# w_out of blocks 2 and 3 as one product of seven block products, in a stated order

## The chip, the cores and the metric

The kernel runs on one core of one Trainium2 chip. The metric is the device time of one launch in microseconds (us). Below, PE is the tensor engine (matmuls and transposes), ACT the scalar engine, DVE the vector engine, POOL the GpSimd engine and SP the sync engine, whose queue issues nearly all transfers (DMA). Matrix operands lie in SBUF as tiles of 128 partitions; matmuls accumulate in PSUM, of which the kernel uses four tiles of two banks at a time.

## The reference, cut to what matters

One layer of a hybrid decoder block on x of 2048 rows by 1024 columns, float32:

```
h   = rmsnorm(x, norm_mix_g)
u   = h @ w_in                                   # 1024 -> 3584 columns
gate_b, gate_c, v, x_r, g = split(u)             # 512, 512, 512, 1024, 1024
y_conv = gate_b * conv3(gate_c * v)              # 512 columns
y_rnn  = rg_lru(conv4(x_r)) * gelu(g)            # 1024 columns, a scan over the rows
y   = concat[rmsnorm(y_conv, g_norm_conv), rmsnorm(y_rnn, g_norm_rnn)]
x   = x + y @ w_out                              # 1536 -> 1024 columns
h   = rmsnorm(x, norm_mlp_g)
x   = x + relu(h @ w_mlp_in)^2 @ w_mlp_out       # 1024 -> 4096 -> 1024
out = rmsnorm(x, final_norm_g)
```

Each rmsnorm divides a row by the root of its mean square, so y_conv and y_rnn each carry one factor per row (rA and rB below) beside the gain per column.

## The kernel before

**Numbers.** Each float32 operand is split into a rounded high part and a low part (`split_into`: ACT copies to the high part, line 177, DVE subtracts it for the low part, line 178). A product of two operands is three matmul passes, high by high, high by low, low by high (`passes`).

**Blocks and pairs.** The 2048 rows are four blocks of 512 rows, in two pairs: blocks 0 and 1, then blocks 2 and 3. A large product over a pair can be computed as seven block products in place of eight: the two blocks are the two row halves, and the other two dimensions are halved as well; some operands are then sums and differences of quarters. The order of the seven is (1, 2, 6, 5, 7, 3, 4) throughout (`ORDER`). The kernel before does this for both MLP products of each pair (classes `Up`, line 838, and `Down`, line 956) and for w_in in the second pair (class `In`, a subclass of `Up`, so its matmuls stand at line 838 too).

**First pair.** For blocks 0 and 1 the mixers are computed one after the other (`mixers`), each followed by `w_out_rows` (the y_rnn part of y @ w_out) and `w_out_conv` (the y_conv part). Both run at line 259, in groups of row tiles of 128 rows. Weight splits are written to DRAM (`put_by`, `cache`) and read back later. While the first pair runs, a background generator, `prepare_sums`, makes the sums of quarters of w_in that the second pair needs, a piece at each call of `step`: its DVE operations are at lines 1236 to 1247 and at 178, and the results go to DRAM. Calls of `step` stand in `col_unit`, in the first pair's up products, and in its down products as long as the number s of the 1024-row slice is below 3.

**Second pair.** `mixers2` runs the 49 products of w_in (steps n = 0 to 48, seven for each of x0, g0, x1, g1, c, v, b) with the recurrence in eight chains beside them (class `Chain`: conv, split, gates, tanh, decay, scan, times, out, add; a chain starts every four steps). In `out`, ACT squares a finished y_rnn tile and the tile is sent to DRAM on the ACT queue (`spill_y`, line 1311). The first chain's `out` is in step 12, the last one's in step 40; sums of squares go to accA and accB. After step 48 follow, block by block, `w_out_rows(2)`, `w_out_conv(2)`, `w_out_rows(3)` and `w_out_conv(3)`: y tiles are read back, split with their gain (`split_y`, lines 579 and 580), multiplied, and the result is added to x as `x += po * r` with the row factor rB (line 1579) or rA (line 1607). A row factor comes from `stats`, matmuls of the sums of squares with a column of ones (line 599), and a few small operations on DVE and one on ACT (`rstd_of`).

**Row norm and turn.** A row tile whose x is complete is normed for the MLP by `norm_tile`: two squares with accumulation on ACT (line 395), small DVE operations, a root on ACT (line 377), more small ones, two multiplications on DVE (line 401). `turn` then transposes the tile with eight PE transposes (line 1586) and ACT copies it out. From the transposed tiles come the MLP's row operands: H1 and H2 from block 2 (`split_first`), H5 and H6 from both blocks (`rest`), later H7, H3 and H4 (`later_operands`).

**What sets the order.** In `mixers2` PE, ACT and DVE run in the order of the program (`manual_schedule` names the three). In `w_out_conv` of the last block of a pair and in the MLP only PE is so ordered. Everywhere else, and for the SP queue always, a planner orders the instructions by program order and readiness when the kernel is built. Each engine executes its own list in order.

Of the kernel before, what the change touches and what calls it, by code (L numbers as in the profile page):

```python
# [1 line left out]

# [12 lines left out]
P = 128  # L15
SEQ = 2048
D = 1024
# [46 lines left out]
def block_kernel(  # L64
# [28 lines left out]
    sp = ctx.enter_context(tc.tile_pool(name="sp", bufs=4))  # L93
    dp = ctx.enter_context(
# [1161 lines left out]

    def step():
        with tc.issue_after(made_at["sp"]):
            next(background, None)
# [17 lines left out]
    def mixers2(b, H, rest):  # L1277
# [9 lines left out]
        yB = [[None] * 4 for _ in range(2)]  # L1287
        stt, ts, tt = V.scalar_tensor_tensor, V.tensor_scalar, V.tensor_tensor
# [25 lines left out]
        class Chain:  # L1314
# [143 lines left out]
        def complete(at_n, kind, k, f, n, t, ps):  # L1458
# [33 lines left out]
            else:  # L1492
# [7 lines left out]
                yA[n][pr] = spill_y(u)  # L1500
# [16 lines left out]
        last = PORDER[-1]  # L1517
        for n in range(-IN_AHEAD, len(seq)):
# [10 lines left out]
            pieces = todo.pop(n, [])  # L1529
            for fn, *args in pieces:  # L1530
                fn(*args)
# [3 lines left out]
            if nm == last and i == 7:  # L1535
                ready = [split_y(refill("y", yB[0][pr]), "g_norm_rnn", 2 * pr) for pr in range(2)]
            if nm == last and i == 3:
                load_unit(cursor[0])
                load_x(b, (0,))
            if nm == last and i == 4:  # L1540
                load_x(b, (1,))
        halves = [[acc[0][:, n : n + 1, :] for n in range(2)] for acc in (accA, accB)]
        return yA, [ready + yB[0][2:], yB[1]], *halves

    def w_out_rows(b, ysB, accB, during, late=None):
        po = [psum("po") for _ in range(NT)]
        held = []
        for pr in range(4):
            w = take("oB%d" % pr, ahead=1 if pr == 1 else OUT_AHEAD)
            y = ysB[pr]  # L1550
            if pr < 2:
                y2 = ysB[pr + 2]
                if b >= PAIRED:
                    y2 = refill("y", y2)
                ysB[pr + 2] = split_y(y2, "g_norm_rnn", 2 * pr + 4)
# [8 lines left out]
            if pr == 1 and late:  # L1564
                late(po[3].rearrange("p h (k q) -> p (h k) q", q=P))
# [52 lines left out]
    background = prepare_sums()  # L1618
# [47 lines left out]

    for b in range(0, NB, 2):
        if b < PAIRED:
# [23 lines left out]
            ysA, ysB, accA, accB = mixers(b + 1, h, early)  # L1692
        else:
            xr0, xr1, xt2 = hs["r"]

            def rest(n):
                if n == 0:
                    half_gates(0)
                    split_pair(5, xr0[:2])
                if n == 22:  # L1700
                    half_gates(1)
                later_operands(n + 3, xr0, xr1, xt2)

            with tc.manual_schedule(
                engines={nc.tensor.engine, nc.scalar.engine, nc.vector.engine}
            ):
                yA2, yB2, rA2, acc2 = mixers2(b, H, rest)
            elsewhere.clear()
            ysA = []

            def during(pr):
                if pr > 1:
                    ysA.append(split_y(refill("y", yA2[0][pr - 2]), "g_norm_conv", 2 * pr - 4))

            w_out_rows(b, yB2[0], acc2[0], during)
            ysB = [refill("y", d) for d in yB2[1][:2]]
            load_x(b + 1)
            raw0 = [temp("raw0") for _ in range(4)]
            ysB = [split_y(y, "g_norm_rnn", 2 * pr) for pr, y in enumerate(ysB)] + yB2[1][2:]
            xs = w_out_conv(b, ysA, stats(rA2[0], 512, "A"), 2, lambda t, xs: turn(xs, t, raw0))  # L1720
            ysA = [refill("y", d) for d in yA2[1]]
# [201 lines left out]
```

## Time and profile before

| | us |
|---|---|
| median of 3 runs (lowest to highest) | 2144.68 (2143.64 to 2146.54) |
| the profiled execution, its own time | 2147.37 |
| span of that execution, first to last instruction | 2145.6 |
| PE busy | 2119.6 |
| DVE busy | 1557.5 |
| ACT busy | 1065.8 |

The profile lists instructions with the time from the start of the span. Overlapping matmuls count once in a busy time, and one matmul's own duration (about 390 ns for 512 columns) is longer than the distance between two of them, since they are pipelined. A line such as "PE tps L1586 <- DVE xs L401: 6.9, 1, 6.9" says that line 1586 on PE stood idle once, for 6.9 us, until line 401 on DVE was done. A "windows" row gives, for a stretch of time, the busy time of each engine, the clock that PE was granted (1.00 is full) and the share of the DMA engines' time that was in use.

In the profiled execution w_in of the second pair runs from 1087.44 to 1376.96 us, w_out of blocks 2 and 3 from there to 1525.94 us, and the second pair's MLP to the end; between 1525.94 and 1538.59 us the last two turns stand between up products. The first pair's down products run from 782.80 to 1087.44 us.

### The profile page before, as it was taken

How to read it: one execution, taken by the hardware profiler on the slowest of the kernel's cores; microseconds unless marked ns; L12 is line 12 of the kernel's file. 1: busy time of each engine (PE TensorE's matmuls, PEld its weight loads, DVE VectorE, ACT ScalarE, POOL GpSimd, SP SyncE). 2: the span in 40 equal slices, each digit the busy share in tenths (PEclk: the TensorE clock that was granted, in tenths of full speed). 3: DMA queues.
4: the chain of work that ended last, by engine and by line, in shares of the span. 5: the costliest groups of instructions: out<-in, count | busy, mean ns of one | idle time of the engine just before them, and what ended most of it. 6: DMA issues, size and time to landing. Idle time of an engine off the chain costs nothing.

```text
span 2145.6 us, 25180 instructions
## 1 busy us (share of the span) xinstructions
PE 2119.6 (99%) x9464; PEld 1742.9 (81%) x9464; DVE 1557.5 (73%) x1826; ACT 1065.8 (50%) x1376; POOL 41.8 (2%) x62
## 2 busy tenths in 40 slices
PE   9999999999999999999999999989999999999998
PEld 7888888788888888888887777878888888888886
DVE  6889547858766779988985678534876666887776
ACT  6884357626555545433456686213564333333344
POOL 0000000000000000000000100000000000000000
PEclk9999999999999999999999999999999999999999
DMA  9988988752577678764384547866335355844432
GB/s 332 325 316 297 337 327 324 276 180 99 186 275 274 244 280 328 283 211 145 112 319 167 186 177 246 322 245 257 115 128 187 118 191 201 326 164 154 135 124 79
DMA packets 197721, 482.48 MB, mean 225 GB/s; under 512 B 15200, under 2 KB 79712, under 8 KB 197600
## 3 DMA queue, kind: packets, MB, share of 16 engines
q1 hardware_dynamic: 195328, 474.07, 61.2%
q10 hardware_dynamic: 2272, 6.82, 0.8%
q8 instruction: 74, 1.21, 0.2%
q14 instruction: 47, 0.39, 0.1%
HBM read 324.59 MB, written 156.24 MB: 224 GB/s over the span
## 4 chain that ended last, share of the span: by engine, by line
PE 87%; DVE 6%; ACT 4%; DMA 2%; issue 1%; SPq 0%; POOL 0%; ACTq 0%; DVEq 0%; POOLq 0%
PE up L838 37%; PE dn L956 27%; PE po L259 12%; PE ps_x L232 2%; PE ps_g L232 2%; PE ps_c L232 1%; PE tps L1586 1%; PE dn L975 1%; DVE v L705 1%; ACT gi L681 1%; DVE xr L638 1%; PE start_x L499 1%; ACT r L678 1%; PE start_x L232 1%; PE start_g L232 1%
## 5 line engine op out<-in xcount | busy, mean ns | idle before, releaser
L838 PE MATMUL up<-H,w_hi 128*128 128x512 f32 x2576 | 796.2, 390 | 3.9 <-ACT xr_in L1467 3.7
L838 PEld LDWEIGHTS up<-H,w_hi 128*128 128x128 f32 x2576 | 482.7, 188 | 109.3 <-issue 4.4
L838 PE MATMUL up<-H,w_lo 128*128 128x512 f32 x1288 | 501.7, 389 | 0.0
L956 PE MATMUL dn<-w_hi,z_hi 128*128 128x512 f32 x864 | 336.1, 389 | 0.0
L956 PE MATMUL dn<-w_lo,z_hi 128*128 128x512 f32 x864 | 336.1, 389 | 0.0
L956 PE MATMUL dn<-w_hi,z_lo 128*128 128x512 f32 x864 | 336.1, 389 | 0.0
L838 PEld LDWEIGHTS up<-H,w_lo 128*128 128x128 f32 x1288 | 242.1, 188 | 50.9 <-DVE w_lo L178 0.3
L177 ACT CAST z_hi<-z 128x1024 fp32r<-128x1024 f32 x112 | 118.1, 1054 | 326.5 <-PE dn L956 283.0
L178 DVE TENSOR_TENSOR w_lo<-w,w_hi 128x1024 fp32r<-128x1024 f32 x156 | 190.0, 1220 | 90.5 <-PE dn L956 36.7
L177 ACT CAST w_hi<-w 128x1024 fp32r<-128x1024 f32 x156 | 162.7, 1049 | 156.4 <-PE up L838 63.9
L956 PEld LDWEIGHTS dn<-w_hi,z_hi 128*128 128x128 f32 x864 | 162.2, 188 | 33.7
L956 PEld LDWEIGHTS dn<-w_hi,z_lo 128*128 128x128 f32 x864 | 162.2, 188 | 33.6
L956 PEld LDWEIGHTS dn<-w_lo,z_hi 128*128 128x128 f32 x864 | 162.2, 188 | 33.5
L178 DVE TENSOR_TENSOR z_lo<-z,z_hi 128x1024 fp32r<-128x1024 f32 x112 | 136.3, 1217 | 21.0 <-ACT z_hi L177 21.0
L988 DVE TENSOR_TENSOR x<-dn,x 128x1024 f32<-128x1024 f32 x108 | 131.6, 1219 | 23.2 <-PE dn L956 20.2
L259 PE MATMUL po<-w_lo,y_hi 128*128 128x512 f32 x384 | 119.3, 392 | 1.2 <-DVE w_lo L178 1.2
L259 PE MATMUL po<-w_hi,y_hi 128*128 128x512 f32 x384 | 120.1, 396 | 0.3 <-DVE ys_B L607 0.3
L259 PE MATMUL po<-w_hi,y_lo 128*128 128x512 f32 x384 | 119.7, 393 | 0.0
L259 PEld LDWEIGHTS po<-w_lo,y_hi 128*128 128x128 f32 x384 | 72.6, 189 | 17.1 <-DVE w_lo L178 1.7
L259 PEld LDWEIGHTS po<-w_hi,y_lo 128*128 128x128 f32 x384 | 72.5, 190 | 15.5 <-DVE y_lo L580 0.4
L259 PEld LDWEIGHTS po<-w_hi,y_hi 128*128 128x128 f32 x384 | 71.6, 190 | 14.6 <-DVE ys_B L607 0.5
L850 ACT COPY snap<-up 128x1024 f32<-128x1024 f32 x48 | 48.7, 1014 | 63.0 <-PE up L838 62.6
(344 smaller groups left out, 2962.1 us busy)
## 6 DMA issues: line engine op xcount, KB each, us to landing
z<-d_z SPq DMA_DIRECT2D x112, 512.0 KB, 4.7
w_hi<-d_w SPq DMA_DIRECT2D x79, 512.0 KB, 6.6
w_lo<-d_w SPq DMA_DIRECT2D x79, 512.0 KB, 6.1
w<-in_w_mlp_in_dram SPq DMA_DIRECT2D x64, 512.0 KB, 5.8
d_z<-snap SPq DMA_DIRECT2D x64, 512.0 KB, 3.2
d_z<-z SPq DMA_DIRECT2D x48, 512.0 KB, 3.4
w<-in_w_mlp_out_dram SPq DMA_DIRECT2D x48, 512.0 KB, 6.0
d_w<-w_hi SPq DMA_DIRECT2D x40, 512.0 KB, 6.2
```

The lines of the kernel that those rows point to most:

```text
L177: nc.scalar.copy(hi, src)
L178: return (lo_engine or V).tensor_tensor(lo, src, hi.bitcast(F32), SUB).ins
L232: nc.tensor.matmul(ps[:, j, lo:hi], ws[k // 4][:, k % 4, j * P : (j + 1) * P], hs[:, k, lo:hi], start=k == 0 and i == 0, stop=k == KD - 1 ...
L259: nc.tensor.matmul(ps[:, half, :], ys[:, j, t * P : (t + 1) * P], ws[j][:, 0, half * 512 : (half + 1) * 512], start=first and i == 0, stop ...
L499: nc.tensor.matmul(start_x[:, j], w[a][k // 4][:, k % 4, j * P : (j + 1) * P], h[c][:, k], start=k == 0 and n == 0, stop=k == KD - 1 and n ...
L638: V.scalar_tensor_tensor(xr[:, j, :], xr_in[:, j, k : k + TB], par("rnn_conv_w", 8 * k + c), xr[:, j, :], MUL, ADD,)
L678: nc.scalar.activation(r[own, j, :], pr_[own, e, :], AF.Sigmoid, bias=par("b_a", c)[own])
L681: nc.scalar.activation(gi[own, j, :], pr_[other, e, :], AF.Sigmoid, bias=par("b_x_swapped", c)[other])
L838: nc.tensor.matmul(ps[:, j, :], ws[:, k, j * P : (j + 1) * P], hs(k), start=i in (1, 2, 5) and k == 0 and n == 0, stop=k == 3 and n == len ...
L850: nc.scalar.copy(t, ps)
L956: nc.tensor.matmul(ps[t // 2][:, t % 2, :], zs[:, p, t * P : (t + 1) * P], ws[:, p, :], start=i in (1, 2, 5) and a == 0 and p == 0 and n == 0,
L988: V.tensor_add(xt[b, th, dh], ps[th], xt[b, th, dh])
```

## The change

The 1536 columns of y for blocks 2 and 3 times w_out become one product of seven block products. The row halves are the blocks, the halves of the inner dimension are three groups of 256 each (`OUT_ROWS`: two of y_rnn, one of y_conv), the output is halved into 512 columns. One block product is 4 row tiles x 3 groups x 2 x 3 passes = 72 matmuls of 512 columns, so the seven are 504, where the four functions before had 576.

- Since sums over both parts of y need one factor per row, y_conv is multiplied by rA/rB (computed as rA * rB * (mean square of y_rnn + eps)), spread over the partitions by a matmul (`diagonal`, `spread`), and the whole result is added to x with rB. The gains go into the tiles themselves: for y_rnn in `Chain.out`, two ACT multiplications in place ahead of the transfer; for y_conv together with the row factor.
- The sums of w_out for products 4 to 7 are made by a second background generator, `prepare_out_sums`, after the first one; four more calls of `step` are allowed, in the first two products of s = 3.
- `pair_before_mlp` holds everything from `mixers2` to the MLP with PE, ACT and DVE in program order. The factor rB of both blocks is computed in step 42, y is read back in steps 44 and 45, and the first splits are in steps 46 to 48. The y_conv tiles stay in SBUF.
- Norms and turns move: block 2's norms into product 3, its turns into product 7, block 3's norms and H1, H2 and the first two MLP weight splits into product 4; all four turns of block 3 go between the first up products of the MLP (`turns_at`), where two were.

The new functions and the changed places, cut:

```diff
-    for b in range(NB):
-        for nm in UNITS if b < PAIRED else ():
+    for b in range(PAIRED):
+        for nm in UNITS:
...
+    OUT_ROWS = (("oB0", "oB1", "oA0"), ("oB2", "oB3", "oA1"))
+    def prepare_out_sums():
...
+        for g in range(3):
+            b12, b11 = load(g, 0, 1), load(g, 0, 0)
+            yield
+            b22 = load(g, 1, 1)
+            yield
+            t3 = temp("t3", W)
+            tt(t3, b22, b12, SUB)
+            tt(b12, b12, b11, SUB)
+            yield
+            tt(b22, b22, b12, SUB)
+            hi = split(t3)
+            yield
+            put(7, g, hi, t3)
+            b21 = load(g, 1, 0)
+            hi = split(b12)
+            yield
+            put(5, g, hi, b12)
+            tt(b21, b21, b22, SUB)
+            hi = split(b22)
+            yield
+            put(6, g, hi, b22)
+            hi = split(b21)
+            yield
+            put(4, g, hi, b21)
...
                 s, v = s_of.pop(self.key), v_of[self.key]
                 square(s, v)
+                for j in range(2):
+                    nc.scalar.activation(
+                        s[:, j, :], s[:, j, :], AF.Copy, scale=par("g_norm_rnn", 2 * pr + j)
+                    )
                 yB[n][pr] = spill_y(s)
...
-                yA[n][pr] = spill_y(u)
+                yA[n][pr] = u
...
-    background = prepare_sums()
+    background = chain(prepare_sums(), prepare_out_sums())
...
+    class WOut:
+        def load(self, i, g):
+            row = []
+            for n in range(2):
+                t = wtile("w_o", (P, 2, TB), F32R)
+                if i > 3:
+                    nc.sync.dma_start(t.bitcast(F32), out_sums[i, g][n])
...
+        def split(self, i, g, src):
+            if g < 2 and i != 4:
+                hi, lo = self.hold[:, g], self.hold[:, 2 + g]
+            else:
+                hi, lo = temp("y_hi", dt=F32R), temp("y_lo", dt=F32R)
+            split_into(hi, lo, src)
+            self.y[i, g] = hi, lo
+        def multiply(self, i, t, ps, gs, first, final):
+            n = 0
+            for g in gs:
+                for j in range(2):
+                    for k, (ys, ws) in enumerate(passes(self.y[i, g], self.w[i, g])):
+                        n += 1
+                        nc.tensor.matmul(
+                            ps[t // 2][:, t % 2, :],
+                            ys[:, j, t * P : (t + 1) * P],
+                            ws[:, j, :],
...
+        def add(self, i, t, ps, rB):
...
+            V.scalar_tensor_tensor(xv, ps[t // 2][:, t % 2, :], rB[:, c : c + 1], xv, MUL, ADD)
...
+    def pair_before_mlp(b, ups):
...
+        def rest(n):
...
+            if n == 42:
+                ps = psum("sps", (P, 2 * NT))
+                stats_pair(st["accB"][0], ps)
+                st["rB"], st["aB"] = rstd_pair(ps, D, "B")
+            if n in (44, 45):
+                for pr in range(4):
+                    y[n - 44, pr // 2, pr % 2] = refill("y", st["yB"][n - 44][pr])
+            if n == 46:
+                o.home(1)
+                o.split(1, 0, y[0, 0, 0])
+                load(2)
+            if n == 47:
+                o.split(1, 1, y[0, 0, 1])
+                load(2)
+            if n == 48:
+                o.home(2)
+                o.split(2, 0, y[0, 1, 0])
+                load(2)
+        mixers2(b, H, rest, st)
...
+        def sums(g):
+            s1[g] = temp("s1")
+            tt(s1[g], y[1, 0, g], y[1, 1, g], ADD)
+            tt(y[1, 0, g], y[0, 0, g], y[1, 0, g], SUB)
+        def more_sums(g):
+            tt(y[0, 0, g], s1[g], y[0, 0, g], SUB)
+            tt(y[0, 1, g], y[0, 1, g], y[0, 0, g], SUB)
+        def scale(n, k, row):
+            t = y[n, k, 2]
+            for j in range(2):
+                V.scalar_tensor_tensor(
+                    t[:, j, :], t[:, j, :], par("g_norm_conv", 2 * k + j), row, MUL, MUL
+                )
+        X = [psum("wo_x") for _ in range(2)]
+        B = (0, 1)
+        for t in range(2):
+            o.multiply(1, t, X, B, True, False)
+        Y = [None, psum("wo_y")]
+        side = Y[1][:, 1, :]
+        stats_pair(st["accA"][0], side[:, : 2 * NT])
+        load_x_half(b, 0)
+        o.split(2, 1, y[0, 1, 1])
+        for t in range(2, NT):
+            o.multiply(1, t, X, B, True, False)
+        sums(0)
+        q, _ = rstd_pair(side[:, : 2 * NT], 512, "A")
+        V.tensor_mul(q, q, rB)
+        V.tensor_mul(q, q, aB)
+        diag = diagonal(q[:, :NT], NT)
+        Y[0] = psum("wo_y")
+        for t in range(2):
+            o.multiply(2, t, Y, B, True, False)
+        load(2)
+        sums(1)
+        diag2 = diagonal(q[:, NT:], NT)
+        spread(diag, NT, side)
+        o.multiply(2, 2, Y, B, True, False)
+        for k in range(2):
+            scale(0, k, side)
+            o.split(1 + k, 2, y[0, k, 2])
+        for t in range(NT):
+            o.multiply(1, t, X, (2,), False, True)
+            o.add(1, t, X, rB)
+        spread(diag2, NT, side)
+        for k in range(2):
+            scale(1, k, side)
+        for t in range(3):
+            o.multiply(2, t, Y, (2,), False, True)
+            o.add(2, t, Y, rB)
+        load(2)
+        more_sums(0)
+        o.home(6)
+        o.split(6, 0, y[0, 0, 0])
+        o.multiply(2, 3, Y, range(3), True, True)
+        o.add(2, 3, Y, rB)
+        sums(2)
+        more_sums(2)
+        o.split(6, 2, y[0, 0, 2])
+        more_sums(1)
+        o.split(6, 1, y[0, 0, 1])
...
+        G = (0, 2, 1)
+        def product(i, ps, gs, first, behind):
+            for t in range(NT):
+                o.multiply(i, t, ps, gs, first, True)
+                o.add(i, t, ps, rB)
+                behind(t)
...
+        product(6, X, G, False, lambda t: prepare(5, s1, t))
+        product(5, Y, range(3), True, lambda t: prepare(3, of(0, 1), t))
...
+        def in_third(t):
+            prepare(7, of(1, 0), t)
+            norm(b, t)
+        product(3, Y, range(3), False, in_third)
...
+        def in_seventh(t):
+            prepare(4, of(1, 1), t)
+            turn(xs[t], t, raw0)
+        product(7, X, range(3), False, in_seventh)
+        ups[0].load((0,))
+        hw = first_operands()
+        def in_fourth(t):
+            norm(b + 1, t)
+            split_first(hw, t, raw0[t])
+            if t > 1:
+                ups[0].prepare(ORDER[t - 2])
+        product(4, X, range(3), False, in_fourth)
...
-            if more and n > 6 and s < NS // 2 - 1:
+            if more and n > 6 and (s < NS // 2 - 1 or i in (1, 2)):
                 step()
...
+                mlp(b, ups, r0, r1, t2, rest, xs, {0: (0, 1), 1: (2,), 2: (3,)}, 2)
```

`stats_pair` and `rstd_pair` do for the eight row tiles of both blocks what `stats` and `rstd_of` do for four. `prepare(i, src, t)` loads three weight pieces and takes a new tile for the splits when t is 0, and splits group t of product i when t is below 3.

More of the change, by code (lines that the diff above doesn't have):

```diff
@@ L1 @@
 from contextlib import ExitStack
+from itertools import chain
 import concourse.bass as bass
@@ L1528, in mixers2 @@
             drain(n, p, nm[0], k, i)
[L1529 to L1530 removed]
+            for fn, *args in todo.pop(n, ()):
                 fn(*args)
@@ L1534, in mixers2, with w_out_rows @@
                 fn(*args)
[L1535 to L1545, printed above, removed]
+    def w_out_rows(b, ysB, accB, during):
         po = [psum("po") for _ in range(NT)]
@@ L1667, in block_kernel @@
     for b in range(0, NB, 2):
+        ups = [Up(s, b < PAIRED) for s in range(NS)]
         if b < PAIRED:
@@ L1869, in block_kernel @@
[L1869 to L1875 removed]
+                xs, r0 = pair_before_mlp(b, ups)
+            r1, t2, rest = turns(r0)
+            with tc.manual_schedule(engines={nc.tensor.engine}):
+                mlp(b, ups, r0, r1, t2, rest, xs, {0: (0, 1), 1: (2,), 2: (3,)}, 2)
```

450 lines of the change are left out of this document (273 added, 177 removed).

## The prediction

> **What bounds the kernel now.** I read the page's head first, then the chain of waits in order of time, the waits of PE, windows over the stages that change, and the timelines of the single engines there.
>
> ```profile
> span 2145.6 us, 25180 instructions
> PE 2119.6 (99%) x9464; PEld 1742.9 (81%) x9464; DVE 1557.5 (73%) x1826; ACT 1065.8 (50%) x1376; POOL 41.8 (2%) x62
> ...
> PE tps L1586 <- DVE xs L401: 6.9, 1, 6.9
> PE up L838 <- ACT xr_in L1467: 3.7, 1, 3.7
> ```
>
> PE is busy for all but 26 us, and the two longest waits are in the stages that change. The chain, in order of time (start, length, what):
>
> ```profile
> 1149.55 1.02 ACT s L1511
> ...
> 1163.40 1.23 DVE s L1389
> 1165.79 1.28 ACT L1473
> ...
> 1218.42 1.02 ACT xr_in L1467
> 1219.49 17.98 PE up L838 x72
> ...
> 1316.90 60.06 PE up L838 x264
> 1376.96 8.16 PE po L259 x36
> ...
> 1434.36 2.73 DVE y_lo L580 x4
> 1440.56 1.94 PE tps L1586 x8
> ...
> 1525.94 5.44 PE up L838 x24
> 1532.25 5.46 PE up L838 x24
> 1538.59 293.78 PE up L838 x1296
> ```
>
> It is PE nearly throughout, so time is saved by taking work from PE or by shortening a wait of PE, and not elsewhere. The last row prices a matmul: 293.78 / 1296 = 0.2267 us. (The 390 ns that the groups show for one is its own pipelined length.) From 1149.55 to 1219.49 the chain is on ACT and DVE: there the recurrence sets the pace, up to PE's wait of 3.7 us.
>
> ```profile
> core 0: us, PE busy (x) PEld busy (x) DVE busy (x) ACT busy (x) POOL busy (x), PEclk, DMA share, GB/s
> 905.00:1033.00 128.00, 128.00 (x566) 106.01 (x566) 105.90 (x95) 48.97 (x49) 0.00 (x0) 1.00 0.55 187
> 1033.00:1087.00 54.00, 54.00 (x240) 44.74 (x239) 48.77 (x66) 26.32 (x49) 0.00 (x0) 1.00 0.41 140
> 1351.00:1376.00 25.00, 25.00 (x112) 20.72 (x111) 13.40 (x16) 6.92 (x9) 0.00 (x0) 1.00 0.94 351
> 1377.00:1526.00 149.00, 141.84 (x657) 118.14 (x656) 67.45 (x155) 40.99 (x98) 0.00 (x0) 0.98 0.64 239
> 1436.00:1450.00 14.00, 9.44 (x42) 8.20 (x43) 7.33 (x21) 2.49 (x9) 0.00 (x0) 0.76 0.44 166
> ```
>
> The w_out stage (fourth row) loses 7 us of 149 on PE, with DVE less than half busy. In the last row PE waits and then runs at half clock for a while (mean grant 0.76 over 14 us).
>
> **Removed: 72 matmuls.** 576 - 504 = 72, times 0.2267 = 16.3 us off PE. [...] The trace has 226.7 ns over 1296 matmuls, and that is used.
>
> **Removed: the wait at the turn.** At 1440.56 PE had waited 6.9 us for a normed tile that stood behind the y_lo splits on DVE. All row norms move behind other products, so it goes. A turn of eight transposes takes 0.87 us (1525.94 + 5.44 to 1532.25) and here took 1.94, and the 24 matmuls behind it were slow too: about 1.9 us lost to the half clock. Together 8.8 us. What is late next is the subject of the next two parts.
>
> **Added: DVE sums ahead of product 6.** The durations:
>
> ```profile
> 1592.26 1.22 DVE L810 TENSOR_TENSOR w<-w,w 128x1024 f32<-128x1024 f32 x1
> 1593.40 1.22 DVE L895 TENSOR_TENSOR z<-snap,z 128x1024 f32<-128x1024 f32 x1
> L442 DVE SCALAR_TENSOR_TENSOR xT<-xT,prm,bcs 128x512 f32<-128x512 f32 x24 | 17.2, 743 | 1.0 <-DMA xT<-in_x_t_dram 0.9
> L177 ACT CAST w_hi<-w 128x1024 fp32r<-128x1024 f32 x156 | 162.7, 1049 | 156.4 <-PE up L838 63.9 <-DVE w_lo L178 34.9 <-DMA w<-in_w_mlp_in_dram 20.8
> 189.51 1.41 DVE L442 SCALAR_TENSOR_TENSOR xT<-xT,prm,bcs 128x512 f32<-128x512 f32 x2
> ```
>
> A DVE operation of 1024 columns costs 1.14 us (distance of the first two rows); one of 512 with a scalar 0.67 in a run (two in 1.41, with 0.07 of overlap at the end); an ACT split 1.05. Products 1 and 2 take 144 matmuls. I follow the written order from the first `spread`. DVE then has, until the last split of product 6 (group 1): eight `scale` operations, seven `add` and one more, 16 x 0.67 = 10.7; five low splits, six operations of `more_sums`, two of `sums`, 13 x 1.14 = 14.8; two waits of 1.25 for ACT's high part behind `scale`, and 0.7 in dependent steps: 28.7 us. PE has (2, t=2) 12, (1, group 2) 24, (2, group 2) 18, (2, t=3) 18 matmuls and a spread, 16.8 us, and then 14 matmuls of product 6's first row tile, 3.2 us. Product 6 goes row tile by row tile through all three groups, so PE must wait for the last group already in the first tile: 28.7 - 20.0 = 8.7, say 8.8 us, in pieces. From both sides: 6 if DVE starts 2 to 3 us earlier against PE, 11 if ACT or a transfer delays it. DVE is busy throughout, so this is a count, not a guess; I take 8.8. Products 5, 3 and 7 need one split and one add per row tile (1.8 us of DVE in 4.08 of PE), in product 3 a norm as well; no wait.
>
> **Added: the way into the MLP.** In product 4 each row tile is followed by its norm, a split of H and, for the third and fourth, a split of an up weight. A row tile in the old stage:
>
> ```profile
> 1448.90 1.41 DVE L1607 SCALAR_TENSOR_TENSOR x<-po,yr_A,x 128x512 f32<-128x512 f32 x2 [5.86 <-PE po L259]
> 1451.10 0.16 DVE L398 TENSOR_TENSOR ss<-ss 128x1 f32<-128x1 f32 x1 [0.79 <-ACT xs L395]
> ...
> 1452.56 1.42 DVE L401 SCALAR_TENSOR_TENSOR xs<-x,rs,gain 128x512 f32<-128x512 f32 x2
> ...
> 1511.53 1.42 DVE L401 SCALAR_TENSOR_TENSOR xs<-x,rs,gain 128x512 f32<-128x512 f32 x2
> ...
> 1517.60 1.41 DVE L401 SCALAR_TENSOR_TENSOR xs<-x,rs,gain 128x512 f32<-128x512 f32 x2
> ```
>
> From the add to the end of the norm 5.1 us, with DVE waiting for ACT's squares in between. In the new order nothing may fill that gap: one add less is -0.7, the squares now wait for the add, +0.7, the H split +1.14: about 6.3 us per tile, against 4.08 on PE. (The two rows of block 3 stand 6.07 us apart, with other work between.) First add at 4.3 us into product 4, third tile's H split at 4.3 + 3 x 6.3 = 23.2, the first up weight's low part at 24.3; PE ends product 4 at 16.3 and can do two matmuls of the up product before it needs that part. Wait: 7.6 us, and 0.3 before the second up product: 7.9. From both sides: 0 if tiles took 4.1, 11 if they took 7.3. I take 7.9.
>
> **Half clock.** After each of these two waits PE may run at half clock for a few us. Taken 1.7 together, between 0 and 3.8 (twice the 1.9 above). [...]
>
> **Added in mixers2.** `out` gets two ACT multiplications, and the transfer on ACT's queue now waits for them:
>
> ```profile
> L1063 ACT ACTIVATE x<-x,fs_r 128x512 f32<-128x512 f32 x16 | 10.7, 714 | 2.7 <-DVE fs_r L1055 2.7
> 1164.70 1.06 ACT L1295 ACTIVATE v<-s 128x1024 f32<-128x1024 f32 x1 [0.59 <-DVE s L1389]
> 1164.73 0.35 ACTq L1311 DMA_DIRECT2D d_y<-s  x1
> 1344.83 0.69 DVE L1304 TENSOR_TENSOR acc<-acc,v 128x512 f32<-128x512 f32 x1
> 1384.96 0.95 PE L599 MATMUL po<-ones_r,acc 128*128 128x1 f32 x8
> 186.29 0.40 PE L432 MATMUL po<-diag_hi,ones_r 128*128 128x512 f32 x1
> 186.53 0.40 PE L432 MATMUL po<-diag_lo,ones_r 128*128 128x512 f32 x1
> ```
>
> The first `out` (1164.70) lies in the chain: 1.34 for the two and about 0.4 for the issue (0.35), which no longer runs beside the square, delay what is behind them on ACT (the gelu at 1165.79) and lengthen the 3.7 us wait by 1.8. Later ones fall mostly into idle ACT time; I add 0.6. Together 2.4, between 0 and 4.2 (as much again as the first).
>
> In step 42 PE must wait for accB: the last add ends at 1345.5, product 42 at 1344.2, and ACT's delay of step 36 shifts the add by up to 1: 1.3 to 2.3, taken 2.0. The eight ones-matmuls are as many as before (0.95 per four tiles). The row factor's small operations fall into idle DVE time (13.40 of 25 busy from 1351), the first splits too. The two spreads cost PE 4 x 0.24 = 0.95.
>
> **Transfers and the first pair.** From step 44 to product 1, eight y tiles and up to twelve weight tiles of 0.5 MB are wanted where DMA already runs at 0.94; before, some eighteen were loaded there without a wait. 0 to 3, taken 0.3; SP's order is the planner's. The MLP's start gets two more turns' worth of DVE work, 2 x 2.7 us, with some 10 us in hand before H7 is needed: 0 to 3, taken 0.2. `prepare_out_sums` gives DVE 24 operations, 27.4 us, and ACT 12.6, behind the sums of w_in, which end at about 905 us. DVE's idle time is 22.1 us up to 1033 and 5.2 more up to 1087: it just fills. Operands are prepared two products (10.9 us) ahead, so I take 1.0, between 0 and 6. Fewer readbacks and the dropped y_conv transfers are worth nothing to PE.
>
> **Sum.** -16.3 - 8.8 + 8.8 + 7.9 + 1.7 + 2.4 + 2.0 + 0.95 + 0.3 + 0.2 + 1.0 = +0.15 on the span of 2145.6, that is, nothing. The profiled execution's own time, 2147.37, is 2.7 above the median of the runs, 2144.68; the difference is put on the median: **2145 us**.
>
> **Rivals.** Faster: the tiles of product 4 overlap better than strict order suggests, so that a tile takes DVE about 4.5 us and the wait before the MLP is 1 or less. For it: DVE is idle for 1.7 us in each tile. Against it: nothing in the list can be moved there. It decides from about 5.2 us per tile down; -7: 2138.
>
> Slower: DVE is full in the first pair's second half. If the 27.4 us come at the wrong places, DVE's lag passes the 10.9 us lead and PE waits, or H operands of the second pair come late. Place: 905 to 1110 us; for it: 27.4 wanted, 27.3 free; against it: DVE was 25 to 27 of 27 us busy from 809 on beside the first sums, with no wait. It decides when more than some 5 us spill over: +6 to +9: 2152.
>
> Slower, second: every `out` delays its chain by 1.8, not only the first, and PE follows ACT through the recurrence: up to +5: 2150. Against it: ACT has idle stretches of 1 to 3 us in each period after 1219.
>
> [...]
>
> **Chances.** No change that this kernel's measurement can tell (within 0.2%, 4.3 us): 0.36. Faster as in the first rival, also by smaller waits at product 6: 0.26. Slower by the first pair 0.21, by the chains 0.15, by the page's rule 0.02, together 0.38. The range, 2135 to 2156, takes in the rival cases with the ends of the half clock and of product 6 beyond them; the forecast's own is 2140.5 to 2149.
>
> **What would show it.** Right: PE matmuls down by 72 less the spreads; no wait at the turns; PE waiting for splits on DVE within the first row tile of product 6 (6 to 11 us) and for a weight split at the first up product (6 to 10), both with a lower granted clock behind; the wait near 1219 at 5 to 6 us; a wait of about 2 us before the ones-matmuls in step 42; DVE near 27 of 27 us from 905 to 1087 with PE still full. Wrong: PE idle in the first pair's down products, weights of w_out arriving late, or PE waiting less than 3 us at either of the two places.

## The result, and the profile after

The changed kernel took 2174.62 us in the median (four runs, 2170.74 to 2180.24), the kernel before in runs beside it 2144.84. The ratio is 1.014 with a 95% interval of 1.0117 to 1.0164. It is slower, and well outside the predicted range of 2135 to 2156. The profiled execution took 2175.13 us for a span of 2173.3.

First the head of its page, then PE's waits (engine, what was done, what it waited for: us in total, times, longest).

```profile
span 2173.3 us, 25139 instructions
PE 2123.4 (98%) x9396; PEld 1736.2 (80%) x9396; DVE 1612.7 (74%) x1865; ACT 1093.4 (50%) x1399; POOL 48.7 (2%) x62
...
PE wo_x L1777 <- DVE x L1790: 9.5, 7, 3.6
PE wo_x L1777 <- ACT y_hi L179: 6.8, 2, 4.2
PE up L840 <- ACT xr_in L1528: 4.3, 1, 4.3
PE wo_w L1777 <- DVE x L1790: 3.9, 4, 1.3
PE dn L958 <- DVE w_lo L180: 3.5, 2, 2.2
PE wo_y L1777 <- DVE x L1790: 3.1, 2, 2.3
PE sps L1720 <- DVE acc L1361: 1.4, 1, 1.4
```

PE has 68 instructions less and is busy for 4 us more: the matmuls that are left ran in part at a lower clock (a mean grant of 0.90 in the stage of w_out, below). The wait at the turn is gone. In its place stand thirteen waits for L1790, the `add` that takes a row tile out of PSUM. The prediction has no such wait.

Where the time came in is read from the chain of waits, at four points that both kernels pass. After:

```profile
472.09 2.95 PE up L840 x13
...
780.06 228.49 PE dn L958 x1008
...
1388.97 5.44 PE wo_x L1777 x24
...
1551.77 5.46 PE up L840 x24
...
1571.70 288.33 PE up L840 x1272
```

and before, the two rows that the prediction does not have:

```profile
475.65 5.44 PE up L838 x24
...
782.80 293.76 PE dn L956 x1296
```

| stretch | before, us | after, us | difference |
|---|---|---|---|
| start to the first up product of the first pair | 475.65 | 472.09 | -3.6 |
| to its first down product (782.80; after: 780.06) | 307.15 | 307.97 | +0.8 |
| to the first matmul of w_out (1376.96; 1388.97) | 594.16 | 608.91 | +14.8 |
| to the fourth up product of the second MLP (1538.59 + 5.44; 1571.70) | 167.07 | 182.73 | +15.7 |
| to the end | 601.6 | 601.6 | 0.0 |

The first row is code that did not change; over all kernels below it lies between 471.0 and 476.0, so it says nothing. The loss is in two stretches of like size: the first pair's second half with the second pair's recurrence, and the stage of w_out, for which the prediction's terms make about 5 us less instead of 15.7 more.

The stage of w_out, after, in windows (width, busy time and operations of PE, PEld, DVE, ACT and POOL, granted clock, DMA):

```profile
1407.00:1451.00 44.00, 30.02 (x92) 20.22 (x90) 26.63 (x30) 6.62 (x7) 0.00 (x0) 0.77 0.38 137
...
1389.00:1552.00 163.00, 138.78 (x558) 107.11 (x558) 92.59 (x157) 39.32 (x76) 0.00 (x0) 0.90 0.44 161
```

The whole stage (second row): PE is idle for 24.2 us, and a mean clock of 0.90 over 163 us takes another 16. The first row is the stretch that the prediction followed operation by operation, from the first spread to the last split of product 6. It has "DVE is busy throughout" there. DVE was busy for 26.6 us of 44.

What held PE up shows in the timelines of PE and DVE (start, length, engine, line, operation, idle time before it and who ended it):

```profile
1410.43 1.41 DVE L1868 SCALAR_TENSOR_TENSOR u<-u,prm,wo_y 128x512 f32<-128x512 f32 x2 [3.38 <-PE wo_y L1777]
...
1418.65 1.22 PE L1777 MATMUL wo_x<-w_o,y_hi 128*128 128x512 f32 x2 [2.30 <-DVE x L1790]
...
1474.42 3.04 PE L1777 MATMUL wo_w<-w_o,y 128*128 128x512 f32 x12 [0.84 <-DVE x L1790]
1483.74 3.06 PE L1777 MATMUL wo_w<-w_o,y 128*128 128x512 f32 x12 [0.84 <-DVE x L1790]
...
1502.87 3.06 PE L1777 MATMUL wo_w<-w_o,y 128*128 128x512 f32 x12 [1.34 <-DVE x L1790]
...
1544.99 1.22 PE L1777 MATMUL wo_x<-w_o,y_hi 128*128 128x512 f32 x2 [3.64 <-DVE x L1790]
```

In products 5 and 3 PE runs 18 matmuls, waits 0.84, runs 36, waits 0.84, runs 36. The wait comes after row tiles 0 and 2 and never after 1. `multiply` and `add` address `ps[t // 2][:, t % 2, :]`: row tiles 0 and 1 are the two banks of one PSUM tile, and so are 2 and 3. The matmuls of row tile 1 write a bank that nobody reads, and wait all the same until `add` has read the other one. The first row is the same the other way round: the scaling reads `side`, a bank of the PSUM tile into whose other bank product 2's row tile 2 is being multiplied, and DVE stands for 3.38 us until those twelve matmuls are done. That suggested the first experiment.

### The profile page after: what moved, and what is told of

It is laid out like the page before. It is cut to its first block, busy times and chain, and to the rows that moved or that the text cites. A ratio compares the mean times of both kernels' runs of the same rounds, so it can differ in the third digit from the quotient of the medians.

```text
span 2173.3 us, 25139 instructions
## 1 busy us (share of the span) xinstructions
PE 2123.4 (98%) x9396; PEld 1736.2 (80%) x9396; DVE 1612.7 (74%) x1865; ACT 1093.4 (50%) x1399; POOL 48.7 (2%) x62
## 4 chain that ended last, share of the span: by engine, by line
PE 80%; DVE 12%; ACT 5%; issue 2%; DMA 2%; SPq 0%; POOL 0%; ACTq 0%; DVEq 0%; POOLq 0%
PE up L840 34%; PE dn L958 25%; PE po L261 5%; PE wo_x L1777 3%; PE ps_g L234 3%; PE ps_x L234 2%; PE ps_c L234 1%; PE wo_w L1777 1%; PE wo_y L1777 1%; DVE v L707 1%; PE tps L1631 1%; DVE x L1790 1%; DVE v L1438 1%; DVE w_lo L180 1%; PE start_x L501 1%
## 5 line engine op out<-in xcount | busy, mean ns | idle before, releaser
L180 DVE TENSOR_TENSOR w_lo<-w,w_hi 128x1024 fp32r<-128x1024 f32 x156 | 189.9, 1219 | 79.2 <-PE dn L958 28.3
L857 ACT ACTIVATE snap<-snap 128x1024 f32<-128x1024 f32 x33 | 35.0, 1062 | 67.7 <-DVE snap L877 26.7
L180 DVE TENSOR_TENSOR w_lo<-raw,w_hi 128x1024 fp32r<-128x1024 f32 x44 | 53.1, 1217 | 11.3 <-ACT w_hi L179 8.7
L261 PE MATMUL po<-w_lo,y_hi 128*128 128x512 f32 x192 | 59.3, 390 | 0.9 <-DVE w_lo L180 0.9
L261 PE MATMUL po<-w_hi,y_hi 128*128 128x512 f32 x192 | 59.6, 392 | 0.0
L261 PE MATMUL po<-w_hi,y_lo 128*128 128x512 f32 x192 | 59.4, 390 | 0.0
L180 DVE TENSOR_TENSOR w_lo<-t,w_hi 128x1024 fp32r<-128x1024 f32 x32 | 39.1, 1221 | 23.5 <-PE dn L958 16.4
```

The source lines that it names most:

```text
L180: return (lo_engine or V).tensor_tensor(lo, src, hi.bitcast(F32), SUB).ins
L261: nc.tensor.matmul(ps[:, half, :], ys[:, j, t * P : (t + 1) * P], ws[j][:, 0, half * 512 : (half + 1) * 512], start=first and i == 0, stop ...
L857: nc.scalar.activation(t, t, AF.Relu)
```

## The experiments

All times are medians; the kernel before had 2144.4 to 2145.9 in the runs beside them. "Stage of w_out" is the fourth stretch of the table above.

### Regrouped banks

```
-  ps[t // 2][:, t % 2, :]      (in multiply and in add)
+  ps[t % 2][:, t // 2, :]
```

> Edit: row tiles 0 and 2 of a product share a PSUM tile, and 1 and 3, where 0 and 1, and 2 and 3 shared one. Theory A (the two banks of one PSUM tile are waited for as one: the add of an even row tile holds up the matmuls of the next one, and the scaling of y waits for twelve matmuls that write the other half): the nine gaps of 0.84 us and the two of 2.3 us behind even row tiles go, the scaling starts some 3 us earlier, and PE stays on the full clock up to product 6; 12 to 20 us less than the changed kernel (2175), so 2155 to 2163. Theory B (what PE waits for is the amount of work on DVE, as the prediction counted it; the gaps are only where the waiting shows): the same time is waited in product 6 and ahead of the MLP instead; 0 to 4 us less, 2171 to 2175.

Measured: 2156.34 us (ratio to before 1.0047, 1.0032 to 1.0062), 18.3 less than the changed kernel's 2174.62: theory A. The stage of w_out falls from 182.7 to 164.9 us. PE's waits in it:

```profile
PE up L840 <- ACT w_hi L179: 4.6, 1, 4.6
PE wo_x L1777 <- ACT y_hi L179: 4.2, 1, 4.2
PE wo_x L1777 <- DVE x L1790: 1.8, 1, 1.8
PE wo_y L1777 <- DVE u L1868: 1.6, 1, 1.6
PE up L840 <- DVE w_lo L180: 1.5, 1, 1.5
PE wo_x L1777 <- DVE y_lo L180: 1.1, 2, 0.5
...
1387.00:1532.00 145.00, 130.00 (x564) 103.94 (x563) 93.26 (x157) 39.80 (x77) 0.00 (x0) 0.95 0.50 183
1405.67:1440.10 34.43, 25.54 (x90) 17.75 (x89) 26.41 (x29) 6.57 (x7) 0.00 (x0) 0.89 0.49 177
```

The waits for L1790 fell from thirteen to one. What is left has the sizes that the prediction worked out: up to the last operand of product 6 it is 4.2 + 1.8 + 1.6 + 1.1 = 8.7 us (predicted 8.8), and ahead of the first up product 4.6 + 1.5 = 6.1 (predicted 7.9, with a low end of 0). The way to the 8.7 is not the predicted one: 4.0 of it are waited in products 1 and 2, before product 6. The last row is the stretch from the first spread to the last split of product 6 in this run. It takes 34.4 us where the prediction counted 28.7, and DVE is idle for 8.0 of them. The idle time fell by 9 us, from 24.2 to 15.0; the other half of the gain is the clock (0.95 of 145 us, 7 us lost instead of 16).

### The sums of w_out alone, in the kernel before

```
-  background = prepare_sums()
+  background = chain(prepare_sums(), prepare_out_sums())
-  if more and n > 6 and s < NS // 2 - 1:
+  if more and n > 6 and (s < NS // 2 - 1 or i in (1, 2)):
```

> Edit: the kernel before, with the weight sums of w_out made behind those of w_in and never read; the rest of the program as before. Theory A (DVE becomes full in the second half of the first pair, and PE waits for low parts of down weights, then runs at half clock): 5 to 8 us more than before, 2150 to 2153, with PE idle for some 3 us between 1010 and 1035 and a granted clock below 1 there. Theory B (the prediction's: it just fits): 0 to 2 us more, 2145 to 2147, and the changed kernel lost its time there by something else.

Measured: 2152.02 us (ratio 1.0034, 1.0021 to 1.0047), 7.0 more than before: theory A. From the first down product to w_out its profile has 600.3 us against 594.2, that is 6.1 more. Its windows, and one of the waits:

```profile
905.00:1005.00 100.00, 100.00 (x443) 82.79 (x442) 88.51 (x79) 42.85 (x44) 0.00 (x0) 1.00 0.79 296
1005.00:1040.00 35.00, 31.46 (x131) 25.16 (x130) 34.64 (x31) 14.71 (x16) 7.07 (x1) 0.95 0.54 190
1040.00:1087.00 47.00, 47.00 (x209) 38.94 (x208) 46.54 (x54) 25.57 (x43) 0.00 (x0) 1.00 0.70 264
...
1022.57 0.50 PE L957 MATMUL dn<-w_lo,z_hi 128*128 128x512 f32 x1 [2.21 <-DVE w_lo L179]
```

The place is narrow. Up to 1005 DVE has 11 us to spare, and PE is full on either side; in the 35 us between, DVE has none. From 1009.7 to 1051.8 DVE runs 37 operations without a pause, one every 1.14 us, in the changed kernel:

```profile
1005.86 1.23 DVE L990 TENSOR_TENSOR x<-dn,x 128x1024 f32<-128x1024 f32 x1 [3.53 <-PE dn L958]
...
1016.53 1.22 DVE L1297 TENSOR_TENSOR w_out<-w_out 128x1024 f32<-128x1024 f32 x1
1017.66 1.22 DVE L929 TENSOR_TENSOR w<-w,w 128x1024 f32<-128x1024 f32 x1
...
1021.07 1.22 DVE L180 TENSOR_TENSOR t<-t,sum_hi 128x1024 fp32r<-128x1024 f32 x1
1022.21 1.22 DVE L180 TENSOR_TENSOR w_lo<-w,w_hi 128x1024 fp32r<-128x1024 f32 x1
```

The last row makes the low part that PE waits for; ahead of it the sums of w_out (L1297, sum_hi) alternate with the sums of down weights (L929). Just before, DVE stood idle for 3.53 us with an evacuation at the head of its queue that waited for PE. Nothing behind it on that queue ran in those 3.53 us: the next operation starts at 1007.00, after it.

### The gain in the recurrence

```
-  for j in range(2):
-      nc.scalar.activation(s[:, j, :], s[:, j, :], AF.Copy, scale=par("g_norm_rnn", 2 * pr + j))
```

> Edit: the changed kernel without the two ACT multiplications in the recurrence's last step; it leaves out the gain of the norm of the recurrent half for blocks 2 and 3, so its output is another. Theory A (they lengthen the wait near 1219 and the half clock behind it, and delay accB in step 42): 2 to 5 us less than the changed kernel, 2170 to 2173. Theory B (ACT has room; the wait comes from when the second half's chains start): within 1 us of it.

Measured: 2169.83 us, 4.8 less than the changed kernel: theory A, at its upper end. By the stretches of the profile it is 2.9 less from the first down product to w_out (606.0 against 608.9) and 1.5 less in the stage of w_out. The wait near 1219 is 3.7 again instead of 4.3, and that ahead of the ones-matmuls of step 42 is 0.5 instead of 1.4:

```profile
PE up L840 <- ACT xr_in L1524: 3.7, 1, 3.7
...
PE sps L1716 <- DVE acc L1361: 0.5, 1, 0.5
```

### The low parts of the new sums on POOL

```
-  split_into(hi, src.bitcast(F32R), src)
+  split_into(hi, src.bitcast(F32R), src, nc.gpsimd)
```

> Edit: the changed kernel with the twelve low parts of the new weight sums subtracted on POOL, which is idle there, instead of DVE. Theory A (those operations on DVE are what PE waits behind in the first pair): 13.7 us of DVE are free again, and PE waits there by 3 to 6 us less: 2169 to 2172. Theory B (the waits come from transfers, or from where the steps are issued): within 1 us of the changed kernel. Theory C (POOL at work slows DVE down, or delays the sums): the same or slower, up to 2180.

Measured: 2176.26 us, 1.6 more than the changed kernel, which the intervals can't tell from no change (ratio 1.0143, 1.0126 to 1.016): theory C, without its slower end. Two groups of POOL's operations, then an operation of DVE, then a wait of PE:

```profile
L180 POOL TENSOR_TENSOR w_out<-w_out,sum_hi 128x1024 fp32r<-128x1024 f32 x9 | 31.7, 3531 | 34.7 <-DVE w_out L1305 20.9 <-ACT sum_hi L179 6.4 <-DVE w_out L1297 4.7
L180 POOL TENSOR_TENSOR t<-t,sum_hi 128x1024 fp32r<-128x1024 f32 x3 | 18.2, 6072 | 557.1 <-ACT sum_hi L179 557.1
...
1000.33 3.41 DVE L180 TENSOR_TENSOR w_lo<-w,w_hi 128x1024 fp32r<-128x1024 f32 x1
...
PE dn L958 <- DVE w_lo L180: 6.8, 4, 3.1
```

POOL took 3.5 to 6.1 us in the mean for what DVE does in 1.22, and three DVE operations of 1024 columns between 1000 and 1042 took 3.40 to 3.42. Others took 1.22 still, two of them (1023.24 and 1024.38) while POOL was busy. PE's wait for low parts rose from 3.5 to 6.8. What made the slow ones slow was not shown.

### The gain after the readback

```
   if n == 46:
+      gains(0, (0, 1))          # two ACT multiplications for each y tile
       o.home(1)
...
       o.split(1, 1, y[0, 0, 1])
+      gains(0, (2, 3))
...
       o.split(2, 0, y[0, 1, 0])
+      gains(1, range(4))
```

> Edit, on top of the kernel with regrouped banks (2156): the gain of the norm of the recurrent half is multiplied in on ACT after the tiles are read back (steps 46 to 48) instead of in the recurrence's last step; the same sixteen ACT operations at another place. Theory A (it is the place in the chain that costs, as the run without them showed 4.8 us): 3 to 5 us less, 2151 to 2153; the wait near 1219 is 3.7 again, and the wait ahead of the ones-matmuls of step 42 falls below 1. Theory B (ACT's 11.4 us cost the same wherever they lie, now ahead of the splits of products 1 and 2): 2155 to 2160, with PE waiting for y in product 1.

Measured: 2161.20 us, 4.9 more than with the regrouped banks alone: theory B, and above its range. The stretch up to w_out became 1.2 us shorter, the stage of w_out 5.6 longer:

```profile
1396.77 5.02 ACT L1836 ACTIVATE y<-y,prm 128x512 f32<-128x512 f32 x8
...
1406.49 0.21 ACT L1727 ACTIVATE sA<-aA 128x8 f32<-128x8 f32 x1 [3.76 <-DVE aA L1726]
...
1417.85 1.22 PE L1773 MATMUL wo_x<-w_o,y_hi 128*128 128x512 f32 x2 [3.94 <-ACT y_hi L179]
```

ACT has idle time there (3.76 us ahead of the second last row), but the row factor's square root (second last row) now comes 16 us after the first matmul of w_out, where in the kernel with regrouped banks DVE's next step on it comes 9.5 after. The spread, the scalings and the splits behind it are late, and PE waits 3.94 us more.

### The sums earlier

```
-BG_FROM = 14
+BG_FROM = 6
```

> Edit, on top of the kernel with regrouped banks (2156): the sums start eight up products earlier in the first pair (BG_FROM 6 instead of 14), so that all of them end some 38 us earlier, ahead of the stretch from 1009 to 1037 in which DVE had 24 operations one behind the other. Theory A (the sums cost because the last group of them falls into that stretch): PE has no wait for low parts of down weights there; 4 to 7 us less, 2149 to 2152. Theory B (DVE is full anywhere in the first pair, so the wait only moves): within 2 us of 2156.

Measured: 2156.86 us, against 2156.34 without the edit: inside theory B's bounds. The stretches say more: from the first down product to w_out 2.7 us less, ahead of it 1.0 more, and the unchanged first part 3.9 more, which hides them. PE waits for a low part of down weights twice still (2.4 us in all, at 950 and 962 instead of 1015 to 1036), and once, for 1.8 us, for one of up weights at 741, where it did not wait before. So the wait in part moved, and a small gain was left open, to be tried again below.

### The order from the row factor to product 6

The core of the edit, on top of the regrouped banks:

```
-  for t in range(2):
-      o.multiply(2, t, Y, B, True, False)
-  sums(1)
-  diag2 = diagonal(q[:, NT:], NT)
-  spread(diag, NT, side)
+  o.multiply(2, 0, Y, B, True, False)
+  spread(diag, NT, side)
   o.multiply(2, 2, Y, B, True, False)
   for k in range(2):
       scale(0, k, side)
+  for k in range(2):
       o.split(1 + k, 2, y[0, k, 2])
+  diag2 = diagonal(q[:, NT:], NT)
+  o.multiply(2, 1, Y, B, True, False)
...
+  for t in range(NT):
+      o.multiply(6, t, X, (0,), False, False)
+  sums(1)
+  more_sums(1)
+  o.split(6, 1, y[0, 0, 1])
+  for t in range(NT):
+      o.multiply(6, t, X, (2,), False, False)
...
-  product(6, X, G, False, ...)
+  product(6, X, (1,), False, ...)
```

> Edit, on top of the kernel with regrouped banks (2156): the stated order from the row factor to product 6 is changed: the spread stands behind product 2's first row tile, both scalings of y stand ahead of both splits, sums of groups 0 and 1 are made later and product 6 goes group by group through its four row tiles, so that PE has 24 matmuls for each group whose operand DVE is still making. Theory A (the 8.7 us of waiting there, and the half clock behind it, are a matter of order: DVE's work is hidden by matmuls that were ready): 8 to 14 us less, 2142 to 2148. Theory B (DVE's amount of work there exceeds PE's, as the prediction counted with 28.7 against 20.0): 0 to 4 us less, with the waits at other places.

Measured: 2146.56 us (ratio to before 1.0008, 0.9999 to 1.0018), 9.8 less than with the regrouped banks alone: theory A. The stage of w_out falls from 164.9 to 154.5 us. The waits of 4.2, 1.8, 1.6 and 1.1 us are gone; four of 0.6 to 0.8 and one of 0.2 are what remains there.

### The order around product 4

```
   hw = first_operands()
+  for t in range(2):
+      split_first(hw, t, raw0[t])
   def in_fourth(t):
-      norm(b + 1, t)
-      split_first(hw, t, raw0[t])
-      if t > 1:
-          ups[0].prepare(ORDER[t - 2])
+      if t < 2:
+          split_first(hw, t + 2, raw0[t + 2])
+      if t in (1, 2):
+          ups[0].prepare(ORDER[t - 1])
+      if t < 2:
+          norm(b + 1, t)
   product(4, X, range(3), False, in_fourth)
+  for t in range(2, NT):
+      norm(b + 1, t)
```

> Edit, on top of the kernel with regrouped banks (2156): around product 4, two quarters of the H split stand ahead of it, the others behind its first two row tiles, the up weights' splits behind the second and third, and the norms of row tiles 2 and 3 behind the product. Theory A (the first up product waits for a weight split that stands behind norms it does not need): the 6.1 us wait and the half clock behind it go, 6 to 9 us less, 2147 to 2150. Theory B (the norms are late then, and the turns of row tiles 2 and 3 in the first up products wait instead): 2154 to 2160.

Measured: 2148.96 us (ratio 1.0013, 1.0003 to 1.0022), 7.4 less than with the regrouped banks alone: theory A. PE no longer waits ahead of the first up product, nor for the late norms. The stage of w_out falls to 155.9 us.

### Both orders, then the rest

> Edit: the regrouped banks with both changes of order, the one from the row factor to product 6 and the one around product 4. Theory A (the two waits are apart, and what was saved at each adds up: 9.8 and 7.4 us by the medians, 10.5 and 9.0 by the stage of w_out in the profiles): 2137 to 2140, 5 to 8 us below the kernel before. Theory B (with the first wait gone, DVE or a transfer becomes late at the second place): 2143 to 2147, no faster than before.

Measured: 2137.79 us, ratio 0.997 (0.9959 to 0.9982): theory A, faster than before by 0.3%. The stage of w_out is 145.7 us, 21 less than before the change. Its window and its end in the chain:

```profile
1388.00:1532.00 144.00, 141.03 (x650) 115.13 (x650) 107.80 (x191) 54.41 (x110) 0.00 (x0) 1.00 0.58 211
...
1477.41 4.08 PE wo_x L1777 x18
...
1497.29 16.34 PE wo_x L1777 x72
1513.63 5.44 PE up L840 x24
```

PE is idle for 3 us of 144, at full clock, and product 4 is one piece of 72 matmuls (16.34 / 72 = 0.227). DVE is busy for 107.8 of 144 us: over the stage, its amount of work was not the bound.

```
-BG_FROM = 14                  (with both orders)
+BG_FROM = 6
```

> Edit, on top of both changes of order: the weight sums start eight up products earlier (BG_FROM 6). Theory A (as the segments of the profiles have it: 2.7 us less from the first down product to the last of w_in, 1.0 more ahead of it, the rest of the earlier run's difference being the first 470 us, which differ by 4 us between executions of any of these kernels): 1 to 3 us less than both orders alone. Theory B (by the medians of the earlier run): within 1 us of it, or more.

Measured: 2136.18 us, 1.6 less than both orders, inside theory A's range; but the intervals of the ratios, 0.995 to 0.9975 here and 0.9959 to 0.9982 there, overlap.

```
-  if n == 42:                 (with both orders, BG_FROM = 14)
+  if n == 44:
       ps = psum("sps", (P, 2 * NT))
```

> Edit, on top of both changes of order: the ones-matmuls over accB and the row factor stand in step 44 instead of step 42. Theory A (PE waits there 1.4 us for DVE's last adds and runs at a lower clock behind it): 1.4 to 3 us less than both orders alone. Theory B (the row factor's small operations now delay the sums ahead of product 1): within 1 us of it, or more.

Measured: 2135.09 us, 2.7 less than both orders (ratio 0.9954, 0.994 to 0.9968): theory A. The wait for accB is gone from the list, and so is the half clock behind it: with both orders alone the 144 matmuls behind a wait of 1.39 took 34.39 us, 0.239 each; here the 96 behind the sixteen ones-matmuls take 21.93, 0.228 each. The intervals of the ratios overlap here too, if barely.

> Edit: regrouped banks, both changes of order, the sums eight up products earlier and the row factor in step 44. Theory A (the four places are apart; what each saved adds up): 2132 to 2135, some 10 to 12 us below the kernel before. Theory B (the differences of 1.6 and 2.7 us between the last three runs are within what their intervals leave open, and do not add up): 2135 to 2138.

Measured: 2132.90 us (2132.68 to 2134.06), ratio 0.9942 (0.9928 to 0.9955): theory A. With all five edits (the banks, both orders, the earlier sums, the row factor in step 44) the change is worth 0.6%, some 13 us below the kernel before beside it and 42 below the changed kernel.

## Why the prediction was wrong

The sum came to nothing net, and 29.8 us were lost. Three experiments, each alone, account for that: 18.3 by waits for a PSUM tile's other bank, with the half clock behind them, 7.0 by the sums and 4.8 by the scalings in `out`. The prediction had 0, 1.0 and 2.4 for them. Term by term:

- **72 matmuls, -16.3, and the turn, -8.8.** Right. Nothing hid the gain for good: where few other waits are left (both orders), the stage of w_out is 21.3 us shorter than before. That is 25.1 saved and 1.9 of ones-matmuls that now stand in step 42, less the two spreads (0.95) and the waits left in it (3 us idle); some 1.7 us stay open. The price of 0.227 us per matmul held (16.34 / 72 in product 4, with both orders); no run shows a lower one, for which 0.02 stands among the chances.
- **DVE sums ahead of product 6, +8.8.** Here the prediction failed most. The step that failed is the sentence "DVE is busy throughout, so this is a count, not a guess". In the changed kernel DVE and PE took turns on the two banks of a PSUM tile, and DVE was busy for 26.6 us of 44. Between 1407 and 1451 PE did 92 instructions, about 21 us of work at 0.2267, in 44 us. With the banks regrouped DVE still waited for PE and ACT (busy 26.4 of 34.4 us) and PE worked longer too (25.5 us instead of 20.0, at a mean grant of 0.89). That the difference is 8.7 again is in good part luck. And it was a matter of the order: with another order 3.0 us of it were left.
- **"Products 5, 3 and 7 need one split and one add per row tile; no wait."** Wrong. In products 5 and 3 each even row tile cost 0.84 (once 1.34), in product 7 0.20 in all. The prediction asked when DVE finishes, and not which buffer PE's next matmuls write. The code of `multiply` and `add`, `ps[t // 2][:, t % 2, :]`, had the answer.
- **The way into the MLP, +7.9.** A wait was there, at another place. In the changed kernel it lay inside product 4, 0.84 and 3.64 us, because row tile 3 waited for the add of row tile 2 behind norms, and the first up product then waited for nothing. With the banks regrouped it lay where it was predicted, 6.1 us. DVE's time per row tile was about right (the last two adds of product 4 are 6.06 apart, predicted 6.3).
- **Half clock, +1.7 (0 to 3.8).** Mis-sized nearly ten times: 16 us in the stage of w_out. It was costed behind two waits, and there were many; behind one of 2.29 us the granted clock was 0.50 for 3.4 us (last section).
- **The sums in the first pair, +1.0 (0 to 6).** 6 to 7 us alone, at 1009 to 1037. The total, 27.4 wanted and 27.3 free, was about right; the free time lay ahead of the place. This is the first slower rival, which asked for 6 to 9 us: its price is shown.
- **The scalings in `out`, +2.4 (0 to 4.2).** 4.8 by the medians, 4.4 by the two stretches of the profile. This is the second slower rival, in part; the stretches do not separate the first chain's delay from later ones. The wait near 1219 grew by 0.6 only, not by 1.8.
- **Step 42, +2.0 (1.3 to 2.3).** 1.36 waited, and 1.7 more by half clock behind it, which the prediction did not have here: the 144 matmuls that follow took 34.38 us, where 0.2267 each makes 32.64. Moving it gave 2.7. In the changed kernel:

```profile
1351.23 0.95 PE L1720 MATMUL sps<-ones_r,acc 128*128 128x1 f32 x8
1353.54 1.05 PE L1720 MATMUL sps<-ones_r,acc 128*128 128x1 f32 x8 [1.36 <-DVE acc L1361]
```

The 14.8 us up to w_out come in the main from the sums (6.1), the scalings (2.9, with 0.9 of the wait in step 42) and the rest of step 42: 0.5 waited, 1.7 by half clock, and some 1.9 for its sixteen ones-matmuls, which stood behind the end of this stretch before. Some 1.7 us are left; these were not tried one by one. The faster rival asked that row tiles of product 4 overlap; with the order changed they did.

## What to carry to other kernels

Before interleaving evacuations with the next product's matmuls, ask of every PSUM tile who waits for it as a whole: two row tiles that follow each other belong in different tiles (18.3 us here). Price a wait with its half clock (3.4 us at a grant of 0.50 behind 2.21 us of waiting here, though not in every run), and fill a wait with matmuls that are ready before counting an engine as full (9.8 us here). Work that "just fits" an engine by its total must fit at each place, behind what already heads its queue (7.0 us here).

## What the runs showed of the hardware

**Half the clock after a wait of 2.2 us.** Windows of 1 us around PE's wait from 1021.3 to 1023.5, in the changed kernel:

```profile
1023.00:1024.00 1.00, 0.52 (x2) 0.48 (x3) 1.00 (x2) 0.00 (x0) 0.00 (x0) 1.00 0.91 360
1024.00:1025.00 1.00, 1.00 (x5) 0.77 (x5) 1.00 (x2) 0.00 (x0) 0.00 (x0) 0.75 1.12 248
...
1027.00:1028.00 1.00, 1.00 (x4) 0.73 (x3) 1.00 (x2) 0.00 (x0) 0.00 (x0) 0.54 0.98 356
1028.00:1029.00 1.00, 1.00 (x6) 0.83 (x5) 1.00 (x1) 0.00 (x0) 0.00 (x0) 1.00 0.98 397
```

One wait of 2.21 us brought a grant near half (0.75 and 0.54 in the windows that it begins and ends in, 0.50 between) from about 1024.5 to 1027.9, 3.4 us, starting a microsecond after PE was at work again. A wait of 2.29 us in the stage of w_out did the same (half from 1430.7 to 1434.1). One of 2.63 and one of 2.30 soon behind it made one slow stretch, from 1413.6 to 1423.9. The waits of 4.21 ahead of product 6 and of 3.64 in product 4 made one each, from 1444.3 to 1458.0 and from 1543.3 to 1550.2, which began while PE still stood. These stretches last 3.4, 10.2, 13.7 and 6.8 us, that is one, three, four and two times 3.4.

There is no sharp least length in the runs. Waits of 1.33 and 0.84 brought no half clock in the changed kernel; with the banks regrouped one of 1.81 did and one of 1.65 did not, and the 2.21 us in the first pair brought none there (granted clock 1.00 from 1005 to 1040). In step 42 a wait of 1.36 was enough (half from 1355.6 to 1359.0), between sixteen matmuls of one column; without the gain in the recurrence 0.47 was enough there, with the order up to product 6 changed 1.37 was not, and in step 44 the sixteen without a wait brought none. What decides whether a wait brings half the clock was not shown. The prediction priced it from one wait, of 6.9 us.

**Two banks, one wait.** The 0.84 us is an `add` of 0.75 us and what lies between the two engines (0.02 us ahead of it and 0.04 behind it, by the chain). No run here shows that the banks themselves disturb each other: the wait is one that the program makes for a PSUM tile, and when the tiles are drawn otherwise the waits for L1790 fall from thirteen to one.
